# Low weight parts written by an accumulating DMA instead of a GpSimd subtraction, in a two-layer Hawk/HGRN2 step

## The chip, the cores and the metric

The kernel runs on one core of a Trainium2 chip. The metric is the device time of one execution in microseconds (us). Engines are named as the profile names them: PE (TensorE matmul), PEld (its weight loads), DVE (VectorE), ACT (ScalarE), POOL (GpSimd), SP (SyncE, which issues most DMAs here).

## What is computed

The reference runs one step of a two-layer decoder trunk on 1024 prompt tokens and 8 x 4 sample tokens (1056 in all), model width 1024, in float32:

```
# layer 0 (RG-LRU)
u = rmsnorm(x) @ w_in                  # 1024 -> 2 x 1536: xb and gate
xc = causal_conv(xb)                   # 4 taps
r, ig = sigmoid(blockdiag(xc) + b)     # 16 blocks of 96 x 96 each
h = scan(a, b)                         # h_t = a_t h_(t-1) + b_t, a = exp(-8 softplus(-lam) r)
x = x + (h * silu(gate)) @ w_out       # 1536 -> 1024
# layer 1 (HGRN2, 8 heads of 128 x 128 state)
q, f, v, gate = rmsnorm(x) @ w_in      # 1024 -> 4 x 1024
o = gated linear attention(q, f, v)
x = x + (rms(o) * silu(gate)) @ w_out
y = rmsnorm(x)
```

## The kernel before, in words

Activations lie transposed: features on the 128 partitions, the 1056 tokens along the free dimension, in three chunks of 352. Each float32 operand of a large product is split into a high part, rounded to the PE's fast format (F32R), and a low part, which is what rounding left over. `mm3` (lines 237 to 243) then makes one product out of three matmuls: high weight by high input (L241), high weight by low input (L242), low weight by high input (L243). So every weight block needs a high and a low copy before its matmuls run.

`weights` (L364) prepares a weight matrix in blocks of up to 512 columns: SP loads the block into one of three buffers `raw`, ACT copies it with rounding into one of four buffers `whi` (L376), and an engine subtracts `whi` from `raw` into one of four buffers `wlo` through `subtract` (L319; the instruction is at L321). The default engine is POOL (`G`). With four buffers and two blocks for a 1024-row product, the blocks of the next item are prepared while the present one is multiplied; a `raw` buffer is free for the next load when both its readers are done.

The callers of `weights` are the input products of layer 0 (`project0`, `by_chunk`, and the head `begin`, which names its engines itself), the two partial output products `out` (L623, 8 blocks of 384 columns each, beside loads and stores of the residual stream), `first1` and `ahead` at the end of layer 0, the first two heads of layer 1 (`HC = 2`), and the first part of the last output product. The other six heads go through `seven`, whose `split` (L1423) has its own subtraction on POOL. Two more places split weights by hand: `load` in `out_last` (L657, 18 subtractions on POOL) and the blocks `late` near the end (L1649, 8 subtractions of 384 columns).

The order of the work is made by the class `Flow`: each step is recorded with its engine, an assumed cost and the keys that it reads and writes. A list scheduler plans each of the two halves (layer 0, layer 1) and emits the instructions in the planned order; after that each engine runs its own list strictly in order, waiting on semaphores. The products of the main path keep their written order on PE; smaller PE work and all work of the other engines is placed by the plan. For layer 0 the plan is also improved by a seeded random search over its first 60 us. A changed cost or step therefore moves instructions in other places too.

In layer 1 the first heads overlap on DVE with `build` (L1342) and `add` (L1362, instruction at L1363), which form sums of input parts for `seven`, and with `scale` (L1031), which multiplies the decay factors into queries and keys. `own_gate` (L1058, instruction at L1061) starts a head's chain; `burst1` to `burst4` are its PE work (L1049 is the first). `parted_sum` splits the sums that `build` forms, with a subtraction on POOL (also L321, tiles `t<-R,t` and `t<-tmp,t`).

Of the kernel before, what the change touches and what calls it, by code (L numbers as in the profile page):

```python
# [14 lines left out]
F32 = mybir.dt.float32  # L15
# [3 lines left out]
AF = mybir.ActivationFunctionType  # L19
ALU = mybir.AluOpType  # L20
# [189 lines left out]
def tile_trunk(ctx: ExitStack, tc: tile.TileContext, xT, prm, hc, w0, wg, wo0, w1, wo1, s_in,  # L210
               yT, h_out, c_out, sp_out, ss_out):
    nc = tc.nc
    V, S, G, T, Q = nc.vector, nc.scalar, nc.gpsimd, nc.tensor, nc.sync
# [15 lines left out]
    def pc(name, j, n=1):  # L229
        a = PRM[name][0] + j  # L230
        return P[:, a:a + n]
# [4 lines left out]
    def chunk(c):  # L236
        return slice(c * CH, (c + 1) * CH)
# [56 lines left out]
    with ExitStack() as l0:  # L294
        pl = l0.enter_context(tc.tile_pool(name="l0", bufs=1, reuse_waits="tile"))
        fl = Flow("PE")

        def fixed(name, shape, dt=F32, pool=None):
            return (pool or pl).tile(shape, dt, tag=name, name=name)
# [7 lines left out]
        def dma(dst, src, r=(), w=(), prio=5, kb=180, q=Q):  # L307
            fl.add("SP" if q is Q else "ACT", 0.45, lambda: q.dma_start(dst, src), r, w, prio, kb * (1.0 if r else 0.75))

        def act(n, emit, r, w, prio=5, more=0.0):  # L310
            fl.add("ACT", 0.25 + 0.0007 * n + more, emit, r, w, prio)

        def dve(n, emit, r, w, prio=5, both=False):
            fl.add("DVE", 0.13 + 0.0011 * n, emit, r, w, prio, both=both)

        def pool(n, emit, r, w, prio=5):
            fl.add("POOL", 0.1 + 0.00245 * n, emit, r, w, prio)

        def subtract(e, n, b, x, a, r, w, prio):  # L319

            emit = lambda: e.tensor_tensor(b, x, a.bitcast(F32), op=ALU.subtract)  # L321
            if e is G:
                pool(n, emit, r, w, prio)
            else:
                dve(n, emit, r, w, prio, True)
# [35 lines left out]
            b = 6 * c + 2 * j + i  # L361
            return X[:, b * CH:(b + 1) * CH], ("X", b)

        def weights(src, n, prio=2, e=G, at=None, q=Q, own=()):  # L364

            own = iter(own)
            got = []
            for a in range(0, n, 512):
                m = min(512, n - a)
                raw, *rk = next(own, None) or next(raws)  # L370
                if at:
                    (hi, hk), (lo, lk) = ((o[:, a:a + m], k) for o, k in at)
                else:
                    (hi, hk), (lo, lk) = next(his), next(los)
                dma(raw[:, :m], src[:, a:a + m], (), rk, prio, m / 2, q)
                act(m, lambda hi=hi, raw=raw, m=m: S.copy(hi[:, :m], raw[:, :m]), rk, (hk,), prio)  # L376
                subtract(e, m, lo[:, :m], raw[:, :m], hi[:, :m], (*rk, hk), (lk,), prio)
                got.append((hi, lo, hk, lk))

            def get(k):  # L380
                q = slice((k % 4) * 128, (k % 4 + 1) * 128)
                hi, lo, hk, lk = got[k // 4]
                return hi[:, q], lo[:, q], (hk, lk)

            return get

        def product(w, xs, step=8, more=()):

            ps, pk = next(mm)
            n = len(xs)  # L390
            for s in range(0, n, step):
                ks = range(s, min(n, s + step))

                def emit(ks=ks):
                    for k in ks:
                        mm3(ps[:, :CH], w(k)[:2], *xs[k][:2], k == 0, k == n - 1)

                fl.add("PE", 0.48 * len(ks), emit, (*(q for k in ks for q in (*xs[k][2], *w(k)[2])), *more), (pk,), 1, main=True)
            return ps, pk

        def xcols(c):
            return [(xh[k][:, chunk(c)], xl[k][:, chunk(c)], (("xh", k, c), ("xl", k, c))) for k in range(KD)]
# [217 lines left out]
        def ycols(c):  # L620
            return [(YH[j][:, chunk(c)], YL[j][:, chunk(c)], (("yh", j, c), ("yl", j, c))) for j in range(3)]
# [24 lines left out]
        def out_last(src):  # L646

            blocks = [{} for _ in range(KD)]

            def load(m, k, n, hi, hks, lo, lks, kept=()):  # L650

                raw, rk = next(raws)
                u = 128 * n
                a, b = ("wl", m, 0, k), ("wl", m, 1, k)
                dma(raw[:, :u], wo0[m][:, 768 + 128 * k:768 + 128 * k + u], (), (rk,), 1, u / 2)
                act(u, lambda: S.copy(hi, raw[:, :u]), (rk,), (*hks, a), 1)
                pool(u, lambda: G.tensor_tensor(lo, raw[:, :u], hi.bitcast(F32), op=ALU.subtract), (rk, a), (*lks, b), 1)  # L657
                for i in range(n):
                    q = slice(128 * i, 128 * i + 128)
                    blocks[m][k + i] = hi[:, q], lo[:, q], (a, b, *kept)  # L660

            def tail(k):
                q = slice(2 * CH, 2 * CH + 256)
                return xh[k][:, q], (("xh", k, 2),), xl[k][:, q], (("xl", k, 2),)

            flat = [o.rearrange("p a b -> p (a b)") for o in (gh, gl)]
            for i in (0, 3):
                q = slice(128 * i, 128 * i + 384)
                load(4, i, 3, flat[0][:, q], (("gh", 0), ("gh", 4)), flat[1][:, q], (("gl", 0), ("gl", 4)))
            for m in range(4):  # L670
                for k in (0, 3):
                    spots = []
                    for i in range(2):
                        a = (2 * m + i) * 768 + 128 * k
                        spots += [X[:, a:a + 384], tuple(("X", b) for b in range(a // CH, (a + 383) // CH + 1))]
                    load(m, k, 3, *spots)
            for i in range(3):
                load(5, 2 * i, 2, *tail(3 + i))
            bufs = [next(his) for _ in range(2)], [next(los) for _ in range(2)]
            ring_ = lambda i, a, n: [o for b in bufs for o in (b[i][0][:, a:a + 128 * n], (b[i][1],))] + [[b[i][1] for b in bufs]]  # L680
            for i, k in ((0, 6), (2, 7)):
                load(6, i, 2, *tail(k))
            load(6, 4, 2, *ring_(0, 0, 2))
            load(7, 0, 2, *ring_(0, 256, 2))
            load(7, 2, 4, *ring_(1, 0, 4))
            ms = (4, 0, 1, 2, 3, 5, 6, 7), (4, 0, 1, 2, 3, 5, 6, 7), (6, 7, 5, 4, 0, 1, 2, 3)
            own = [next(xos) for _ in range(NXO)]
            spare = halves[0][:8], own + [halves[0][8]] + [halves[1][i] for i in (0, 3, 6, 1)], halves[0][:8]
            for c in range(NCH):
                acc = next(xbs)  # L690
                rows = []
                for i, m in enumerate(ms[c]):
                    ps, pk = product(blocks[m].get, ycols(c) + xcols(c)[:3], 1)
                    x, xk = spare[c][m]
                    dma(x, src[m][:, chunk(c)], ((2, m, c),), (xk,), 3)
                    dve(CH, lambda x=x, ps=ps: V.tensor_tensor(x, ps[:, :CH], x, op=ALU.add), (pk, xk), (xk,), 0)
                    dma(x1d[m][:, chunk(c)], x, (xk,), (("x1d", m, c),), 3)
                    squares(i, x, xk, acc)
                    rows.append((m, x, xk))
                bc, bk = norm(acc)  # L700
                for m, x, xk in rows:
                    scaled_parts(c, m, x, xk, bc, bk, pc("g1", m), ("P",), G if m % 4 == 3 else V, 4)
# [139 lines left out]
        raw = (halves[1][:8], [slots[i] for i in (1, 4, 7, 2, 5, 8)] + [halves[1][8], free[8]], free[:8])  # L842
# [82 lines left out]
    with ExitStack() as l1:  # L925
        p1 = l1.enter_context(tc.tile_pool(name="l1", bufs=1, reuse_waits="tile"))
        fl = Flow(side=0.4)
# [7 lines left out]
        at = fixed("attn", [128, 8, 128], F32, p1)  # L935
# [634 lines left out]
        for k in range(H):  # L1570
            if k < 4:
                olds = [("x", 1, k, x) for x in range(2)] + [("T", 1, i, k, x) for i in range(2) for x in range(2)]
            else:
                n, i = ((2, 0), (3, 0), (4, 0), (4, 1))[k - 4]
# [21 lines left out]
        own = []  # L1596
# [42 lines left out]
        nl = 128 * K2  # L1639
        late = []  # L1640
        for m in range(KD):
            row = (xh, xl)[m // 4][4 + m % 4]
            hi, lo, hk, lk = row[:, :nl], row[:, nl:2 * nl], ("late", m, 0), ("late", m, 1)
            for k in (hk, lk):
                inherit(k, [("x", p, m % 4, x) for p in (2, 3) for x in range(2)])
            raw, rk = next(raws)
            dma(raw[:, :nl], wo1[m][:, 128 * K1:], (), (rk,), 1, nl / 2)
            act(nl, lambda hi=hi, raw=raw: S.copy(hi, raw[:, :nl]), (rk,), (hk,), 1)
            pool(nl, lambda hi=hi, lo=lo, raw=raw: G.tensor_tensor(lo, raw[:, :nl], hi.bitcast(F32), op=ALU.subtract), (rk, hk), (lk,), 1)  # L1649
            late.append((hi, lo, (hk, lk)))  # L1650

        spare = []
# [54 lines left out]
        for a, n in OUT:  # L1707
            q = slice(a, a + n)
# [3 lines left out]
            for m in range(KD):  # L1712
# [5 lines left out]
                hi, lo, wk = late[m]  # L1718
# [97 lines left out]
```

## Time and profile before

| | |
|---|---|
| median of 3 runs | 1077.81 us (1077.65 to 1078.84) |
| the profiled execution, its own time | 1075.47 us |
| its span | 1073.7 us |
| granted TensorE clock, mean over the span | 0.996 |
| instructions | 25345 |
| busy: PE / PEld / DVE / ACT / POOL | 1053.0 / 1024.5 / 808.2 / 611.1 / 558.0 us |
| DMA | 103.05 MB, mean 96 GB/s |

The page counts an engine as busy from the start of an instruction to its end; matmuls overlap, so one that is 0.32 us long may follow the last after 0.16 us. Line numbers are those of the kernel. A tile's name without a number stands for all its buffers.

### The profile page before, as it was taken

What the parts mean: (1) busy time and instruction counts of PE and PEld (TensorE: products, weight loads), DVE (VectorE), ACT (ScalarE), POOL (GpSimd) and SP (SyncE); (2) the same over time, 40 slices, a digit from 0 to 9 for tenths busy, and PEclk for the clock granted to TensorE, in tenths of its full rate; (3) what the DMA queues carried; (4) which work ended last, traced back from release to release, by engine and by line L of the source; (5) the groups of instructions that cost most, each with busy time, mean ns of one, the idle gap of its engine ahead of it and who ended that gap; (6) DMA issues with size and microseconds to landing.
All of it is one profiled execution on the core that took longest, in us unless ns stands there. A gap on an engine that the chain in (4) does not pass through costs nothing.

```text
span 1073.7 us, 25345 instructions
## 1 busy us (share of the span) xinstructions
PE 1053.0 (98%) x9972; PEld 1024.5 (95%) x9972; DVE 808.2 (75%) x1535; ACT 611.1 (57%) x1395; POOL 558.0 (52%) x546
## 2 busy tenths in 40 slices
PE   9999999999999999999999998999999999999997
PEld 9999999999999999999998997999999999989996
DVE  8999996887997787283999997767768585774446
ACT  7578656867665964243364563747474655752323
POOL 3425353353543547455574854656566665541545
PEclk9999999999999999999999999999999999999998
DMA  9101112124832775240110121212121212354204
GB/s 302 59 27 43 56 49 71 58 61 126 271 104 66 222 252 176 103 131 34 60 51 24 49 92 43 100 43 91 35 92 41 91 44 80 116 169 160 85 1 162
DMA packets 70119, 103.05 MB, mean 96 GB/s; under 512 B 9200, under 2 KB 51184, under 8 KB 70000
## 3 DMA queue, kind: packets, MB, share of 16 engines
q1 hardware_dynamic: 67696, 98.67, 28.1%
q10 hardware_dynamic: 2304, 2.77, 0.8%
q8 instruction: 78, 1.28, 0.5%
q14 instruction: 41, 0.34, 0.1%
HBM read 71.05 MB, written 25.49 MB: 90 GB/s over the span
## 4 chain that ended last, share of the span: by engine, by line
PE 82%; DVE 14%; issue 1%; DMA 1%; ACT 1%; POOL 0%; SPq 0%; POOLq 0%; ACTq 0%; DVEq 0%
PE mm L241 23%; PE mm L242 22%; PE mm L243 22%; PE hg L1049 2%; DVE R L1363 1%; DVE R L1031 1%; PE hg L1266 1%; PE hg L565 1%; DVE tmp L1363 1%; PE hg L1158 1%; DVE a L1232 1%; PE hg L1268 1%; DVE sg L1031 1%; PE hg L241 1%; PE hg L242 1%
## 5 line engine op out<-in xcount | busy, mean ns | idle before, releaser
L241 PE MATMUL mm<-xh,whi 128*128 128x352 f32 (+1 forms) x1143 | 359.3, 314 | 7.2 <-DVE sg L1504 4.5
L242 PE MATMUL mm<-xl,whi 128*128 128x352 f32 (+1 forms) x1143 | 353.2, 309 | 0.0
L243 PE MATMUL mm<-xh,wlo 128*128 128x352 f32 (+1 forms) x1143 | 353.2, 309 | 0.0
L321 POOL TENSOR_TENSOR wlo<-wraw,whi 128x512 fp32r<-128x512 f32 (+2 forms) x131 | 175.9, 1351 | 168.7 <-ACT whi L376 83.6
L241 PEld LDWEIGHTS mm<-xh,whi 128*128 128x128 f32 x1143 | 214.7, 188 | 10.5 <-DVE sg L1504 6.0
L242 PEld LDWEIGHTS mm<-xl,whi 128*128 128x128 f32 x1143 | 215.0, 188 | 1.6 <-DVE xl L321 0.2
L243 PEld LDWEIGHTS mm<-xh,wlo 128*128 128x128 f32 x1143 | 214.9, 188 | 0.0
L497 DVE SCALAR_TENSOR_TENSOR k<-xb,prm_sb,k 128x352 f32<-128x352 f32 (+2 forms) x144 | 90.1, 637 | 10.9 <-ACT k L494 6.1
L241 PE MATMUL mm<-t,whi 128*128 128x264 f32 (+1 forms) x306 | 89.5, 293 | 0.0
L242 PE MATMUL mm<-t,whi 128*128 128x264 f32 (+1 forms) x306 | 87.7, 287 | 0.0
L243 PE MATMUL mm<-t,wlo 128*128 128x264 f32 (+1 forms) x306 | 87.5, 286 | 0.0
L580 POOL TENSOR_TENSOR k<-X 128x352 f32<-128x352 f32 x36 | 44.9, 1256 | 47.8 <-DVE R L581 38.6
L321 POOL TENSOR_TENSOR wlo<-R,whi 128x512 fp32r<-128x512 f32 x33 | 49.9, 1511 | 32.8 <-ACT whi L1423 28.9
L376 ACT CAST whi<-wraw 128x512 fp32r<-128x512 f32 (+2 forms) x83 | 46.0, 574 | 28.5 <-PE mm L242 16.9
L241 PEld LDWEIGHTS mm<-t,whi 128*128 128x128 f32 x306 | 57.6, 188 | 0.7 <-ACT k L1481 0.5
L1504 DVE TENSOR_TENSOR k<-mm,k 128x264 f32<-128x264 f32 x62 | 26.5, 430 | 41.5 <-PE mm L243 41.4
L243 PEld LDWEIGHTS mm<-t,wlo 128*128 128x128 f32 x306 | 57.7, 188 | 0.0
L242 PEld LDWEIGHTS mm<-t,whi 128*128 128x128 f32 x306 | 57.6, 188 | 0.0
L1031 DVE TENSOR_TENSOR R<-R,sg 128x512 f32<-128x512 f32 (+1 forms) x48 | 50.4, 1050 | 0.1
L241 PE MATMUL mm<-yh,whi 128*128 128x352 f32 x153 | 49.9, 326 | 0.0
L243 PE MATMUL mm<-yh,wlo 128*128 128x352 f32 x153 | 49.4, 323 | 0.0
L242 PE MATMUL mm<-yl,whi 128*128 128x352 f32 x153 | 49.4, 323 | 0.0
(415 smaller groups left out, 2684.6 us busy)
## 6 DMA issues: line engine op xcount, KB each, us to landing
wraw<-in_w_dram SPq DMA_DIRECT2D x91, 256.0 KB, 2.6
wraw<-in_wo_dram SPq DMA_DIRECT2D x34, 192.0 KB, 2.5
si<-in_s_in_dram SPq DMA_DIRECT2D x8, 512.0 KB, 4.2
out_ss_out_dram<-si SPq DMA_DIRECT2D x8, 512.0 KB, 2.6
sg<-x1b SPq DMA_DIRECT2D x21, 176.0 KB, 2.8
x<-sg SPq DMA_DIRECT2D x21, 176.0 KB, 1.8
R<-in_w_dram SPq DMA_DIRECT2D x14, 256.0 KB, 2.5
R<-td SPq DMA_DIRECT2D x72, 44.0 KB, 2.0
```

Of the source, the lines that this page charges most:

```text
L241: T.matmul(out, wh, xh, start=first, stop=False, skip_group_check=chained)
L242: T.matmul(out, wh, xl, start=False, stop=False, skip_group_check=chained)
L243: T.matmul(out, wl, xh, start=False, stop=last, skip_group_check=chained)
L321: emit = lambda: e.tensor_tensor(b, x, a.bitcast(F32), op=ALU.subtract)
L376: act(m, lambda hi=hi, raw=raw, m=m: S.copy(hi[:, :m], raw[:, :m]), rk, (hk,), prio)
L497: dve(u, lambda src=src, dst=dst, sh=sh, k=k: V.scalar_tensor_tensor(dst, sh(src, k), pc("cw", 12 * k + m), dst, op0=ALU.mult, op1=ALU.add ...
L565: fl.add("PE", 0.62, lambda ps=ps, i=i, c=c: T.matmul(ps[:96, :CH], gs[:, i, :], ST[:96, chunk(c)], start=True, stop=True), (("gs",), *((" ...
L580: pool(CH, lambda x=x, a=a, b=b: G.tensor_tensor(x, a.bitcast(F32), b.bitcast(F32), op=ALU.add), (ak, bk), (xk,), 3)
L1031: dve(n // 2, lambda sv=sv, dv=dv, s=s, f=f: V.tensor_tensor(dv[:, :, s, :], sv[:, :, s, :], f, op=ALU.mult), (*sk, *gk), dk if i == o els ...
L1049: T.matmul(ps[32 * j:32 * j + 32, n * w:n * w + w], B[:, o:o + 32], q(slice(o, o + 32)), start=True, stop=True, tile_position=(0, 32 * j))
L1363: dve(n, lambda: V.tensor_tensor(o, a, b, op=op), r, (w,), prio, True)
L1504: dve(QT, lambda: V.tensor_tensor(o[0], z[0], u[0], op=ALU.add), (z[1], u[1]), (o[1],), 0)
```

## The change

A new helper `low` replaces the subtraction on POOL in `weights` (where no engine is named) and for the `late` blocks. ACT writes the negated rounded block into the low buffer with one more activation, and POOL issues a DMA that adds the raw block to it in place: raw + (-rounded) is the low part. The DMA is planned at 0.93 us of POOL and half a KB for each column. The blocks of `out_last` keep a subtraction, on DVE instead of POOL. The splits in `seven`, those of the gate weights in `lru` (L543), and those with a named engine stay as they were.

```diff
+        def low(n, dst, src, r, w, prio=5):
+
+            act(n, lambda: S.activation(dst, src, AF.Copy, scale=-1.0), r, w, prio)
+            fl.add("POOL", 0.93, lambda: G.dma_start(dst.bitcast(F32), src, accum_op=ALU.add), (*r, *w), w, prio, n / 2)
+
...
-        def weights(src, n, prio=2, e=G, at=None, q=Q, own=()):
+        def weights(src, n, prio=2, e=None, at=None, q=Q, own=()):
...
                 act(m, lambda hi=hi, raw=raw, m=m: S.copy(hi[:, :m], raw[:, :m]), rk, (hk,), prio)
-                subtract(e, m, lo[:, :m], raw[:, :m], hi[:, :m], (*rk, hk), (lk,), prio)
+                if e is None:
+                    low(m, lo[:, :m], raw[:, :m], rk, (lk,), prio)
+                else:
+                    subtract(e, m, lo[:, :m], raw[:, :m], hi[:, :m], (*rk, hk), (lk,), prio)
...
-                pool(u, lambda: G.tensor_tensor(lo, raw[:, :u], hi.bitcast(F32), op=ALU.subtract), (rk, a), (*lks, b), 1)
+                subtract(V, u, lo, raw[:, :u], hi, (rk, a), (*lks, b), 1)
...
-            pool(nl, lambda hi=hi, lo=lo, raw=raw: G.tensor_tensor(lo, raw[:, :nl], hi.bitcast(F32), op=ALU.subtract), (rk, hk), (lk,), 1)
+            low(nl, lo, raw[:, :nl], (rk,), (lk,), 1)
```

In the program that results, POOL issues 92 such DMAs (60 of 512 columns, 24 of 384, 8 of 128) and ACT runs 92 activations more.

## The prediction

> **What bounds the kernel now.** I read the page first, for its busy times, slices and chain.
>
> ```profile
> PE 1053.0 (98%) x9972; PEld 1024.5 (95%) x9972; DVE 808.2 (75%) x1535; ACT 611.1 (57%) x1395; POOL 558.0 (52%) x546
> ...
> PE 82%; DVE 14%; issue 1%; DMA 1%; ACT 1%; POOL 0%; SPq 0%; POOLq 0%; ACTq 0%; DVEq 0%
> ```
>
> PE is busy in 98% of the span. The change adds and removes no matmul, so it can win at most what PE still waits: 1073.7 - 1053.0 = 20.7 us, and only that part which lies where weight blocks are prepared. POOL, which the change relieves, carries 0% of the chain. Second is DVE with 14%. The next view is the table by stage, then PE's waits.
>
> ```profile
> core 0: us, PE busy (x) PEld busy (x) DVE busy (x) ACT busy (x) POOL busy (x), PEclk, DMA share, GB/s
> ...
> 350.00:400.00 50.00, 50.00 (x305) 48.79 (x304) 41.84 (x66) 40.43 (x69) 25.11 (x19) 1.00 0.79 250
> ...
> 515.00:568.00 53.00, 50.76 (x682) 49.24 (x685) 51.64 (x93) 28.23 (x66) 33.07 (x30) 1.00 0.15 51
> ...
> 616.00:656.00 40.00, 36.09 (x510) 33.97 (x499) 38.36 (x63) 21.65 (x52) 23.31 (x19) 1.00 0.21 76
> ...
> PE hg L1049 <- DVE R L1061: 2.0, 1, 2.0
> ```
>
> In layer 0 (the row 350:400 stands for it) PE has no idle time: nothing can be won there, only lost. From 515 to 568 us, the first two heads of layer 1, DVE is busy in 51.64 of 53 us and PE idles 53 - 50.76 = 2.24 us, of which 2.0 are one wait, for `own_gate` (L1061), the last of a long row of DVE instructions. This is the one place where PE waits for an engine whose work the change touches. From 616 to 656 PE idles 3.91 us behind DVE too, but there POOL serves `seven`, which the change leaves alone.
>
> **What the change gives: DVE loses its collisions with POOL.** POOL's instructions from 515 to 568, grouped, and a few pairs in order of time:
>
> ```profile
> L321 POOL TENSOR_TENSOR t<-R,t 128x264 fp32r<-128x264 f32 x12 | 13.7, 1152 | 10.4 <-ACT t L1366 10.4
> L321 POOL TENSOR_TENSOR wlo<-wraw,whi 128x512 fp32r<-128x512 f32 x7 | 10.8, 1549 | 1.3 <-ACT whi L376 1.3
> L321 POOL TENSOR_TENSOR t<-tmp,t 128x264 fp32r<-128x264 f32 x10 | 9.0, 914 | 7.7 <-ACT t L1366 7.7
> ...
> 524.81 1.29 POOL L321 TENSOR_TENSOR wlo<-wraw,whi 128x512 fp32r<-128x512 f32 x1
> ...
> 525.50 1.17 DVE L1031 TENSOR_TENSOR R<-R,ST 128x528 f32<-128x528 f32 x1
> ...
> 527.25 1.76 POOL L321 TENSOR_TENSOR wlo<-wraw,whi 128x512 fp32r<-128x512 f32 x1
> ...
> 527.77 1.80 DVE L1031 TENSOR_TENSOR R<-R,sg 128x528 f32<-128x528 f32 x1
> ...
> 529.49 0.70 DVE L1031 TENSOR_TENSOR sg<-a,sg 128x528 f32<-128x528 f32 x1
> ...
> 540.61 2.73 POOL L321 TENSOR_TENSOR wlo<-wraw,whi 128x512 fp32r<-128x512 f32 x2
> ...
> 540.77 1.41 DVE L1363 TENSOR_TENSOR R<-xh,R 128x264 f32<-128x264 f32 x1
> ...
> 542.11 1.78 DVE L1031 TENSOR_TENSOR R<-R,sg 128x512 f32<-128x512 f32 x1
> ...
> 553.87 0.69 DVE L1031 TENSOR_TENSOR R<-R,sg 128x512 f32<-128x512 f32 x1
> ...
> 553.97 1.73 POOL L321 TENSOR_TENSOR wlo<-wraw,whi 128x512 fp32r<-128x512 f32 x1
> ...
> 554.48 1.52 DVE L1363 TENSOR_TENSOR R<-R,xh 128x264 f32<-128x264 f32 x1
> ...
> 556.03 0.43 DVE L1363 TENSOR_TENSOR R<-R,xl 128x264 f32<-128x264 f32 x1
> ```
>
> The same DVE instruction takes 0.70 us alone and 1.80 beside a POOL subtraction; at 512 columns 0.69 and 1.78; at 264 columns 0.43 and 1.41 to 1.52. Beside the seven weight subtractions of this stage the rows show these extensions: 1.17 - 0.70 = 0.47, 1.80 - 0.70 = 1.10, 1.41 - 0.43 = 0.98, 1.78 - 0.69 = 1.09, 1.52 - 0.43 = 1.09, together 4.7 us on the engine that sets the pace. The change takes all seven away. The 22 subtractions of `parted_sum` (13.7 + 9.0 us) stay and will go on colliding, perhaps at other instructions, so 4.7 is an upper figure; but PE can use only its own 2.24 us of waiting, under half of it. What is late next is PE itself: behind the gap there is only its own queue of products. Gain: 2.2 us.
>
> **What it costs, each with its cover.** Prices for one block:
>
> ```profile
> L376 ACT CAST whi<-wraw 128x512 fp32r<-128x512 f32 x61 | 36.9, 618 | 28.4 <-PE mm L242 16.9 <-DMA wraw<-in_w_dram 5.1 <-DMA R<-td 3.7
> ...
> L376 ACT CAST whi<-wraw 128x384 fp32r<-128x384 f32 x16 | 7.8, 512 | 0.1
> ...
> L1294 POOL TENSOR_TENSOR rst<-rst,mhalf 128x4 f32<-128x4 f32 (+1 forms) x24 | 21.4, 901 | 22.0 <-DVE rst L1292 22.0
> ...
> wraw<-in_w_dram SPq DMA_DIRECT2D x91, 256.0 KB, 2.6
> ...
> x<-sg SPq DMA_DIRECT2D x21, 176.0 KB, 1.8
> ```
>
> ACT: 60 blocks x 0.62 + 24 x 0.51 + 8 at about 0.3 (an estimate from these two by size) = 52 us. They lie mostly in stages like 350:400, where ACT has 9.6 of 50 us free and the four result banks that PE writes in turn cover a late eviction: a result waits until PE has filled the other three. Charge 0; without that cover each activation costs PE its own 0.6 us.
>
> POOL: the trace holds no DMA issued by POOL. Bounds: SP's issue of a block below (0.38 us, `276.60` further down) and a whole subtraction above, 1.55 us. I take 0.9, the price of POOL's smallest arithmetic instruction (L1294), since most of both is start and end. 92 x 0.9 = 83 us in place of 92 subtractions; POOL is at 52%, so charge 0. Behind the issue, POOL's queue holds the `parted_sum` subtractions and the steps that feed `own_gate`; an issue that waits for ACT's second activation holds them 0.6 us longer, yet it holds POOL itself 0.6 us less.
>
> Landing: the nearest rows are a load of 256 KB, 2.6 us, and a 176 KB transfer out of SBUF, 1.8 us. An accumulating DMA has to fetch the destination as well, so the bounds are 1.8 and twice 2.6 = 5.2; I take 2.6, the same size. A block is then ready later than now by the second activation 0.6 + issue 0.9 + landing 2.6 - subtraction 1.5 = 2.6 us (from 0.6 + 0.4 + 1.8 - 1.5 = 1.3 to 0.6 + 1.5 + 5.2 - 1.5 = 5.8). Does a block have that much time? I followed the 52 blocks that `weights` splits on POOL between 74 and 397 us from their subtraction to their first L243. The row at 321.57 stands for the usual case, and the others are two of the tightest:
>
> ```profile
> 278.26 4.62 POOL L321 TENSOR_TENSOR wlo<-wraw,whi 128x384 fp32r<-128x384 f32 x3 [1.60 <-ACT whi L376]
> ...
> 283.23 0.32 PE L243 MATMUL mm<-yh,wlo 128*128 128x352 f32 x1
> ...
> 321.57 1.53 POOL L321 TENSOR_TENSOR wlo<-wraw,whi 128x512 fp32r<-128x512 f32 x1 [0.87 <-ACT whi L376]
> ...
> 334.16 0.32 PE L243 MATMUL mm<-xh,wlo 128*128 128x352 f32 x1
> ...
> 391.07 1.33 POOL L321 TENSOR_TENSOR wlo<-wraw,whi 128x512 fp32r<-128x512 f32 x1 [0.20 <-ACT whi L376]
> ...
> 396.35 0.32 PE L243 MATMUL mm<-xh,wlo 128*128 128x352 f32 x1
> ```
>
> The usual block is done at 323.10 and used at 334.16, 11 us later. The first of the three subtractions from 278.26 ends near 279.8 (a third of 4.62 us) and its matmul starts at 283.23: 3.4 us. The last ends at 392.40 and is used at 396.35: 3.95 us. Both exceed 2.6: charge 0; at the upper bound 5.8 - 3.4 = 2.4 us and 5.8 - 3.95 = 1.85 us, one behind the other.
>
> DMA traffic: 60 x 256 + 24 x 192 + 8 x 64 KB = 21 MB more, a fifth of the present 103. In most stages that is nothing. In the two output products it is not:
>
> ```profile
> 280.00:290.00 10.00, 10.00 (x65) 10.00 (x64) 9.79 (x12) 2.74 (x5) 5.68 (x4) 1.00 0.97 295
> ...
> 380.00:390.00 10.00, 10.00 (x65) 10.00 (x64) 8.50 (x17) 4.87 (x10) 3.17 (x3) 1.00 0.93 298
> ...
> 390.00:420.00 30.00, 30.00 (x190) 30.00 (x189) 28.56 (x45) 18.55 (x38) 17.45 (x21) 1.00 0.61 193
> ...
> 276.60 0.38 SPq L308 DMA_DIRECT2D xb<-in_xT_dram  x1
> ...
> 285.21 0.49 DVE L632 TENSOR_TENSOR xb<-mm,xb 128x352 f32<-128x352 f32 x1
> ```
>
> The engines move 295 GB/s there at 97% busy. Eight blocks of 192 KB add 1.57 MB: 5.3 us of that capacity, or 10.7 if the fetched destination counts again. The residual load shown is issued at 276.60 and added at 285.21, 8.6 us later, of which it needs about the 2.6 of the load above: 6 us of lateness are covered. Charge 0; at the upper figure 10.7 - 6 = 4.7 us for each of the two products. SP's queue is in order: a load of `raw` waits until the DMA, not the subtraction, has read the buffer, and holds the residual loads behind it for as long.
>
> DVE receives the 18 subtractions of `out_last`, about 0.55 us each (between 0.43 and 0.69 above), 10 us in a stage around 390:420 where it is busy in 28.56 of 30. POOL's 18 end there, and with them extensions of 0.5 to 1.1 each, 9 to 20 us. Charge 0, at most 1 us. The head is planned anew by the random search: 45 of the 48 warm-up matmuls now stand first, 29 before. The work is the same; I give it 1 us in the range, on either side.
>
> [...]
>
> **Sum.** -2.2 + 0 = -2.2 us. The profiled execution took 1075.47 us (span 1073.7 and 1.8 around it), 2.3 below the median of 1077.81; I carry the difference over to the median: 1075.6 us.
>
> **Rivals.**
> 1. *Slower: the accumulating DMA lands late where the DMA engines are full.* Place: the two output products, in the rows 280:290 and 380:390, and the last block of `by_chunk` behind them. For it: 0.97 and 0.93 busy, and the 3.4 and 3.95 us above. Against: the usual block has 11 us. It decides from a landing of about 4 us or added DMA time of 6 us in one product. Price: 4.7 x 2 at the full upper bound of traffic, plus 2.4 + 1.85 of late blocks, 13.7 in all; when it happens half of it is likelier than all, 6.9 - 2.2 = +4.7: 1082.5 us.
> 2. *No change: the DVE stage stays as long as it is.* The 22 remaining subtractions move into the freed POOL time and meet other DVE instructions, or the first blocks of layer 1 come late and PE waits for them instead. It decides if DVE gains less than 2.2 of the 4.7 us. Time: 1077.8.
> 3. *More: DVE's lead beyond PE's need reaches the stage from 616 to 656.* It would have to survive 48 us in which DVE is not always busy; at most the 3.91 us of idle PE time go too. Half of it: 1075.6 - 2.0 = 1073.6.
>
> That the change does not do what it says is excluded: the instruction order holds the 92 DMAs and 92 activations.
>
> **Chances.** 0.2% (2.2 us) is about what a measurement of this kernel can tell from no change. Forecast 0.45: being at that edge, 0.28 of it counts as faster and 0.17 as same. Rival 1: 0.35, all slower. Rival 2: 0.08, 0.07 same and 0.01 slower. Rival 3: 0.12, faster. Faster 0.40, same 0.24, slower 0.36. Range: down to rival 3 with most of its idle time and the head's 1 us, 1072.5; up to rival 1 with its late blocks and most of its traffic, 1086. The forecast's own range is 1073.5 to 1077.5.
>
> **What would show it.** Right: PE's wait for L1061 near 566 gone; L1031 and L1363 on DVE shorter in the mean; PE at 10.00 of 10 in both output products. Wrong: a wait of L243, L241 or a DVE addition (L632 before) for a DMA around these two products, issues on POOL well over 1 us, landings over 4 us.

## The result, and the profile after

The changed kernel takes 1086.01 us (median of 4 runs, 1085.04 to 1087.9) against 1077.73 us before on the same chip (1077.18 to 1078.84): a ratio of 1.0079, 95% interval 1.0063 to 1.0095. It is 8.3 us slower; the forecast was 1075.6, 2.2 faster. The profiled execution of after took 1085.06 us with a span of 1083.2.

The page of after, those lines that answer to the ones of before, with the two largest DMA queues (q0 is POOL's) and the accumulating DMAs' median from issue to landing:

```profile
PE 1059.0 (98%) x9972; PEld 1030.5 (95%) x9972; DVE 767.8 (71%) x1553; ACT 655.7 (61%) x1487; POOL 492.6 (45%) x528
...
q1 hardware_dynamic: 67696, 98.67, 29.4%
q0 software_dynamic: 13248, 20.98, 11.7%
...
PE 85%; DVE 9%; DMA 3%; issue 1%; ACT 1%; SPq 0%; POOL 0%; ACTq 0%; POOLq 0%; DVEq 0%
...
wlo<-wraw POOLq DMA_DIRECT2D x58, 256.0 KB, 4.1
```

DVE and POOL are relieved as meant (808.2 to 767.8 us and 558.0 to 492.6), yet PE is busy 6 us longer with the same 9972 matmuls, and DMA has risen from 1% to 3% of the chain. The table by stage of after:

```profile
core 0: us, PE busy (x) PEld busy (x) DVE busy (x) ACT busy (x) POOL busy (x), PEclk, DMA share, GB/s
280.00:290.00 10.00, 10.00 (x61) 9.52 (x60) 8.03 (x15) 8.07 (x13) 5.20 (x6) 1.00 0.91 244
350.00:400.00 50.00, 48.58 (x292) 46.83 (x291) 29.71 (x55) 41.56 (x73) 15.11 (x17) 1.00 0.91 243
380.00:390.00 10.00, 10.00 (x64) 10.00 (x64) 7.66 (x12) 5.89 (x12) 1.75 (x2) 1.00 1.03 287
390.00:420.00 30.00, 27.90 (x163) 27.36 (x162) 19.89 (x44) 21.86 (x43) 3.40 (x5) 0.94 0.86 246
515.00:568.00 53.00, 53.00 (x671) 51.84 (x670) 44.69 (x93) 29.67 (x69) 27.77 (x32) 1.00 0.51 115
616.00:656.00 40.00, 37.65 (x528) 35.86 (x526) 39.51 (x63) 24.50 (x59) 25.15 (x21) 1.00 0.21 68
```

From 515 to 568 PE now has no idle time: the predicted gain is there. In 390:420, where before had none, PE idles 2.1 us and its granted clock is 0.94. PE's waits in after:

```profile
PE mm L241 <- DVE sg L533: 2.7, 1, 2.7
PE mm L241 <- ACT xh L1598: 2.4, 1, 2.4
PE mm L243 <- DMA wlo<-wraw: 2.1, 1, 2.1
PE mm L241 <- DVE k L1512: 1.7, 1, 1.7
```

and the first two of them before (the last two did not exist):

```profile
PE mm L241 <- ACT xh L1590: 1.4, 1, 1.4
...
PE mm L241 <- DVE sg L525: 1.0, 1, 1.0
```

Waits alone don't show where time is lost for good, so I also took the start of the n-th matmul in each trace, counted from the first one; PE's order is nearly the same in all of these kernels. The difference to the profiled execution of before, in us (its time, 1075.47, was itself 2.3 below its median, so all entries at the end look about 2 us worse than the medians do):

| at (us of before) | 79 | 389 | 405 | 537 | 567 | 655 | 940 | 993 | end |
|---|---|---|---|---|---|---|---|---|---|
| after | 1.6 | 3.9 | 7.9 | 8.2 | 6.0 | 6.9 | 7.1 | 9.8 | 9.9 |
| x1_layer0_sub | 0.1 | 0.1 | 0.1 | 0.0 | -2.3 | -0.5 | -0.4 | 2.4 | 2.9 |
| x2_layer1_sub | 3.5 | 6.3 | 8.5 | 8.8 | 7.8 | 7.6 | 8.0 | 9.4 | 9.9 |
| x3_price | 2.6 | 5.7 | 15.6 | 16.5 | 14.2 | 16.7 | 16.3 | 18.8 | 22.2 |
| x4_copy | 1.5 | 3.8 | 5.1 | 5.3 | 3.2 | 4.0 | 4.2 | 5.3 | 5.9 |
| x5_head1_only | 0.3 | 0.3 | 0.3 | 0.2 | -1.8 | -0.1 | -0.2 | 1.6 | 1.7 |
| x6_bychunk_sub | 5.3 | 7.1 | 7.2 | 7.6 | 5.5 | 6.2 | 6.4 | 9.0 | 9.4 |
| x7_after_seed2 | 1.4 | 3.7 | 7.7 | 7.6 | 5.5 | 7.1 | 7.0 | 10.2 | 10.3 |
| x8_before_seed2 | 3.0 | 4.6 | 4.7 | 5.2 | 5.1 | 5.1 | 5.2 | 5.3 | 5.6 |
| x9_out_sub | 1.1 | 2.9 | 3.0 | 3.5 | 1.3 | 2.0 | 1.9 | 4.3 | 4.4 |
| x10_head1_kb | 0.9 | 0.9 | 0.9 | 0.9 | -1.6 | -0.2 | -0.2 | 1.2 | 1.2 |
| x11_head1_pool | 0.0 | 0.0 | 0.0 | 0.1 | -2.2 | -2.8 | -2.8 | -0.7 | -0.7 |

The row of after splits the 9.9 us: 1.6 in the head; 2.3 between 79 and 389, most of it spread over all matmuls without a wait; 4.0 at one place near 397; 0.3 up to 537; a gain of 2.2 at 566; then 0.9 up to 655, 0.2 up to 940, 2.7 near 950 and 0.1 at the end. The experiments take these one by one.

**The place near 397.** The third block of `by_chunk` in before: its load (SP), its subtraction, and the first L243 that uses it:

```profile
377.93 0.52 SPq L308 DMA_DIRECT2D wraw<-in_w_dram  x1
...
386.24 1.68 POOL L321 TENSOR_TENSOR wlo<-wraw,whi 128x512 fp32r<-128x512 f32 x1 [3.03 <-ACT whi L376]
...
394.44 0.32 PE L243 MATMUL mm<-xh,wlo 128*128 128x352 f32 x1
```

The same block in after:

```profile
389.65 1.27 SPq L308 DMA_DIRECT2D wraw<-in_w_dram  x1
...
394.58 0.64 ACT L312 ACTIVATE wlo<-wraw 128x512 fp32r<-128x512 f32 x1 [0.56 <-DMA wraw<-in_w_dram]
...
395.61 0.87 POOL L313 DMA_DIRECT2D wlo<-wraw  x1 [7.85 <-ACT wlo L312]
...
400.69 0.66 PE L243 MATMUL mm<-xh,wlo 128*128 128x352 f32 x1 [2.10 <-DMA wlo<-wraw]
```

Before, the block was done at 387.92 and had 6.5 us to spare. After, it lands at about 400.6. PE itself is 3.9 us late here, so the block is 400.6 - 387.9 - 3.9 = 8.8 us late against PE. Of that its load is 389.65 - 377.93 - 3.9 = 7.8; the way from load to ready takes only 1.0 longer (11.0 against 10.0). The wait is 2.1 us by the end that the profile gives the matmul before it, and 2.3 counted from start to start, less the usual distance of 0.16. Behind the wait PE's granted clock halves, in windows of 2 us:

```profile
398.00:400.00 2.00, 0.58 (x4) 0.29 (x2) 0.17 (x1) 1.95 (x3) 0.00 (x0) 1.00 1.03 203
400.00:402.00 2.00, 1.31 (x4) 1.32 (x5) 0.00 (x0) 1.69 (x3) 0.00 (x0) 0.63 1.10 308
402.00:404.00 2.00, 2.00 (x8) 2.00 (x8) 0.00 (x0) 1.97 (x3) 0.00 (x0) 0.52 1.02 312
404.00:406.00 2.00, 2.00 (x14) 2.00 (x14) 1.78 (x3) 2.00 (x6) 0.00 (x0) 1.00 0.72 190
```

Eight matmuls in the third row where the fourth has 14. The record of the clock gives 3.413 us at half speed from 400.50 on, which costs half of it, 1.7 us: 2.3 of wait and 1.7 of clock are the 4.0.

### The profile page after: what moved, and what is told of

It is laid out like the page before. It is cut to its first block, busy times and chain, and to the rows that moved or that the text cites. A ratio compares the mean times of both kernels' runs of the same rounds, so it can differ in the third digit from the quotient of the medians.

```text
span 1083.2 us, 25545 instructions
## 1 busy us (share of the span) xinstructions
PE 1059.0 (98%) x9972; PEld 1030.5 (95%) x9972; DVE 767.8 (71%) x1553; ACT 655.7 (61%) x1487; POOL 492.6 (45%) x528
## 3 DMA queue, kind: packets, MB, share of 16 engines
q0 software_dynamic: 13248, 20.98, 11.7%
## 4 chain that ended last, share of the span: by engine, by line
PE 85%; DVE 9%; DMA 3%; issue 1%; ACT 1%; SPq 0%; POOL 0%; ACTq 0%; POOLq 0%; DVEq 0%
PE mm L241 24%; PE mm L243 23%; PE mm L242 23%; PE hg L1057 2%; PE hg L1274 1%; PE hg L1166 1%; DVE a L1240 1%; DMA wraw<-in_w_dram 1%; PE hg L1276 1%; PE hg L573 1%; DVE sg L1039 1%; PE hg L241 1%; PE hg L243 1%; PE hg L242 1%; DVE R L1039 1%
## 5 line engine op out<-in xcount | busy, mean ns | idle before, releaser
L241 PE MATMUL mm<-xh,whi 128*128 128x352 f32 (+1 forms) x1143 | 358.9, 314 | 7.7 <-DVE sg L1512 5.1
L243 PE MATMUL mm<-xh,wlo 128*128 128x352 f32 (+1 forms) x1143 | 355.1, 311 | 2.1 <-DMA wlo<-wraw 2.1
L242 PE MATMUL mm<-xl,whi 128*128 128x352 f32 (+1 forms) x1143 | 354.4, 310 | 0.0
L241 PEld LDWEIGHTS mm<-xh,whi 128*128 128x128 f32 x1143 | 215.3, 188 | 10.6 <-DVE sg L1512 6.6
L243 PEld LDWEIGHTS mm<-xh,wlo 128*128 128x128 f32 x1143 | 215.4, 188 | 2.4 <-DMA wlo<-wraw 2.4
L242 PEld LDWEIGHTS mm<-xl,whi 128*128 128x128 f32 x1143 | 216.0, 189 | 1.3 <-DVE xl L326 0.2
L313 POOL DMA_DIRECT2D wlo<-wraw x80 | 72.0, 946 | 130.8 <-ACT wlo L312 109.2
L326 POOL TENSOR_TENSOR wlo<-wraw,whi 128x512 fp32r<-128x512 f32 x51 | 69.3, 1363 | 66.4 <-ACT whi L1431 53.7
L241 PE MATMUL mm<-t,whi 128*128 128x264 f32 (+1 forms) x306 | 89.6, 293 | 0.7 <-ACT k L1489 0.7
L505 DVE SCALAR_TENSOR_TENSOR k<-xb,prm_sb,k 128x352 f32<-128x352 f32 (+2 forms) x144 | 78.0, 551 | 15.9 <-ACT k L502 8.1
L242 PE MATMUL mm<-t,whi 128*128 128x264 f32 (+1 forms) x306 | 87.6, 286 | 0.0
L243 PE MATMUL mm<-t,wlo 128*128 128x264 f32 (+1 forms) x306 | 87.5, 286 | 0.0
L588 POOL TENSOR_TENSOR k<-X 128x352 f32<-128x352 f32 x36 | 42.0, 1179 | 66.4 <-DVE R L589 61.3
L312 ACT ACTIVATE wlo<-wraw 128x512 fp32r<-128x512 f32 (+2 forms) x80 | 45.4, 585 | 32.8 <-PE mm L243 22.9
L241 PEld LDWEIGHTS mm<-t,whi 128*128 128x128 f32 x306 | 57.5, 188 | 1.2 <-ACT k L1489 0.9
L242 PEld LDWEIGHTS mm<-t,whi 128*128 128x128 f32 x306 | 57.7, 189 | 0.0
L243 PEld LDWEIGHTS mm<-t,wlo 128*128 128x128 f32 x306 | 57.6, 188 | 0.0
L1512 DVE TENSOR_TENSOR k<-mm,k 128x264 f32<-128x264 f32 x62 | 26.3, 428 | 37.1 <-PE mm L243 36.8
L241 PE MATMUL mm<-yh,whi 128*128 128x352 f32 x153 | 51.8, 338 | 0.3 <-DVE k L640 0.3
L243 PE MATMUL mm<-yh,wlo 128*128 128x352 f32 x153 | 49.4, 323 | 0.0
```

The costliest lines, as they stand in the source:

```text
L241: T.matmul(out, wh, xh, start=first, stop=False, skip_group_check=chained)
L242: T.matmul(out, wh, xl, start=False, stop=False, skip_group_check=chained)
L243: T.matmul(out, wl, xh, start=False, stop=last, skip_group_check=chained)
L312: act(n, lambda: S.activation(dst, src, AF.Copy, scale=-1.0), r, w, prio)
L313: fl.add("POOL", 0.93, lambda: G.dma_start(dst.bitcast(F32), src, accum_op=ALU.add), (*r, *w), w, prio, n / 2)
L505: dve(u, lambda src=src, dst=dst, sh=sh, k=k: V.scalar_tensor_tensor(dst, sh(src, k), pc("cw", 12 * k + m), dst, op0=ALU.mult, op1=ALU.add ...
```

## The experiments

**x1_layer0_sub: layer 0 back on POOL's subtraction.**

```
-                if e is None:
+                if e is None and fl.until is None:
                     low(...)
                 else:
-                    subtract(e, ...)
+                    subtract(e or G, ...)
```

`fl.until is None` holds in layer 1's plan alone.

> The blocks that `weights` splits in layer 0 go back to a subtraction on POOL; the accumulating DMA stays in layer 1, and the 18 subtractions of out_last stay on DVE. Matmul by matmul the changed kernel runs behind the one before by 1.6 us at 60 us, 3.9 at 390, 7.8 at 400, 6.0 at 567, 6.9 at 700 and 9.5 at the end. Theory A (the DMAs of layer 0 cost it, where the DMA engines are full): the 3.9 us at 397 and the 2.3 us between 60 and 390 go, the gain of 2.0 at 565 stays: 1086.0 - 6.2 = 1079.8, or 1078.2 if the head's 1.6 goes too. Theory B (layer 1's DMAs cost it, or the 18 subtractions on DVE): 1084 to 1086.

Measured: 1078.0 us (11 runs) against 1078.1, ratio 1.0001, interval 0.9993 to 1.001. The head, the slow spread and the place at 397 are all back to 0.1, so all that was lost up to 400 us came with the accumulating blocks of layer 0 or with the new plan that they bring (x8 tells these two apart); the 18 subtractions of `out_last`, still on DVE, cost nothing (0.1 at 405 and at 485). The gain at 566 is there, 2.3. It is lost again: a wait of 1.9 us (2.1 from start to start) for L1512 at 615 and two spells of half clock, behind 615 and behind 944.

**x2_layer1_sub: layer 1 back on POOL's subtraction.** The condition above turned round, and the last part of the output product through `subtract(G, ...)`.

> The reverse: layer 1's blocks go back to a subtraction on POOL, layer 0 keeps the accumulating DMA. Theory A: the losses up to 400 us stay (+7.8), the gain of 2.0 at 565 goes, and so do the 2.6 us lost around 950: about 1086.0 + 2.0 - 2.6 - 0.8 = 1084.6. Theory B: most of the loss goes, 1080 or less.

Measured: 1085.65 us, ratio 1.0081 (1.0066 to 1.0096). Theory A holds: without layer 1's accumulating DMAs the loss stays. In this trace 3.4 us of it are two spells of half clock, at 33 and 658 us; behind its wait at 400, of 1.9 us from start to start, there is none. Of the gain at 566 half is still there (8.8 to 7.8): PE comes 8 us late and waits 1.0 instead of 2.0.

**x3_price: the planner counts twice the bytes.**

```
-            fl.add("POOL", 0.93, lambda: G.dma_start(..., accum_op=ALU.add), (*r, *w), w, prio, n / 2)
+            fl.add("POOL", 0.93, lambda: G.dma_start(..., accum_op=ALU.add), (*r, *w), w, prio, n)
```

> The same kernel as the changed one, but the planner counts an accumulating DMA with twice the bytes (n instead of n/2 KB), since its packets were measured at 10.3 GB/s on an engine against 20.5 for the others. Theory C (the engines have the room, the planner only put the load of by_chunk's block too late): the wait of L243 for a DMA at 397 goes with its 3.9 us: about 1082. Theory D (no order helps while eight output blocks and by_chunk's blocks share full engines): within 1.5 us of 1086.0.

Measured: 1095.81 us, ratio 1.0169 (1.0155 to 1.0184). Both theories miss: the true price made it 10 us worse. The same block in this kernel, its negation, its issue and PE's wait:

```profile
399.14 0.61 ACT L312 ACTIVATE wlo<-wraw 128x512 fp32r<-128x512 f32 x1
...
400.16 0.87 POOL L313 DMA_DIRECT2D wlo<-wraw  x1 [1.55 <-PE mm L243]
...
407.40 0.66 PE L243 MATMUL mm<-xh,wlo 128*128 128x352 f32 x1 [6.51 <-DMA wlo<-wraw]
```

Its load went out at 391.50, against PE as late as in after (PE is 5.7 behind at 389 here, 3.9 there). What came on top is ACT: in after it negates the block as soon as the load has landed (394.58), here only at 399.14, 7.6 us after the load's issue, behind other work in its list. With the 6.5 us of wait came 10.2 us of half clock, 5.2 of them behind the wait's end. So a planner that thinks the accumulates hold the buffers longer does not load earlier, and the order that it writes for SP and ACT sets how late the block is.

**x4_copy: the same DMA without the add.**

```
-            fl.add(... G.dma_start(dst.bitcast(F32), src, accum_op=ALU.add) ...)
+            fl.add(... G.dma_start(dst.bitcast(F32), src) ...)
```

> The POOL-issued DMA only copies (no accumulate; the low part is then the raw block, so the products are other numbers), everything else including the order is the same. Theory A1 (fetching the destination makes these DMAs slow): the time of a 2 KB packet falls from 178 ns to about 90, landings from 4.1 to about 3 us, and the wait at 397 shrinks from 2.26 us to under 1 and with it the half clock of 3.4 us behind it: 1081 to 1083. Theory A2 (the price is the way through POOL's queue or the buffers it holds, not the add): within 1 us of 1086.0.

Measured: 1083.35 us, ratio 1.0057 (1.0044 to 1.007). Its queue and its landing from its page, and PE's wait at 397 from its waits:

```profile
q0 software_dynamic: 6592, 20.98, 5.2%
...
wlo<-wraw POOLq DMA_DIRECT2D x58, 256.0 KB, 2.6
```

```profile
PE mm L243 <- DMA wlo<-wraw: 0.9, 1, 0.9
```

The same 20.98 MB take 5.2% of the DMA engines instead of 11.7%, land in 2.6 us instead of 4.1, POOL's issue falls from 0.89 to 0.56 us (medians), and the wait falls to 0.9 with no half clock behind it. By the ratios the add is worth 0.0079 - 0.0057 of 1078, 2.4 us; the other 6.1 of the loss are not the add's. SP's list is the same as in after, and the third block's load goes out at 387.14, 2.4 us earlier against PE; that much of its 7.8 is the add's traffic, and the rest is not. In the table this row has the head and the spread of after (1.5 and 3.8) to 0.1 us, though its DMAs are twice as quick.

**x5_head1_only: the kernel before, with the accumulating DMA in head 1's eight blocks alone.**

```
-        def weights(src, n, prio=2, e=None, at=None, q=Q, own=()):
+        def weights(src, n, prio=2, e=G, at=None, q=Q, own=()):
...
-                    ws2[i] = weights(order[i][0], 1024)
+                    ws2[i] = weights(order[i][0], 1024, e=None)
```

with `out_last` and `late` on POOL as before.

> The kernel before, with the negation and the accumulating DMA only in the eight blocks that `weights` splits for head 1 of layer 1, the ones whose subtractions collided with DVE between 515 and 568 us; everything else, out_last too, subtracts on POOL. Theory A: the wait of 2.0 us for own_gate at 566 goes and no block of layer 0 or of the end moves: 2.2 us gained up to 600 us; if no new spell of half clock follows, 1078.1 - 2.2 = 1075.9. Theory E (PE only waits later what it gains there, since DVE is full up to 656, and half-clock spells follow PE's new waits): 1077.5 to 1078.5.

Measured: 1076.38 us (12 runs) against 1077.93, ratio 0.9988 (0.9979 to 0.9996): between the two theories. The gain of 2.1 at 566 is there, and 1.8 of it is waited out at 615:

```profile
618.68 0.39 PE L241 MATMUL mm<-xh,whi 128*128 128x264 f32 x1 [1.67 <-DVE k L1512]
```

DVE was not idle there: it had four sums L1371 in a row in its list ahead of this eviction, where before had one.

**x6_bychunk_sub: only by_chunk's four blocks back on POOL.** `weights(src, 1024, e=G)` in `by_chunk`.

> The changed kernel, with only the four blocks of by_chunk (the last projection of layer 0, loaded while the second output product writes its results) back on POOL's subtraction. Theory A (the accumulating DMA of its block lands too late, 6.0 us there against 4.1 in the middle): the wait of L243 for a DMA at 397 goes with the 2.26 us and the 1.7 us of half clock behind it: 1086.0 - 3.9 = 1082.1. Rival F (the block's load itself is late, held in SP's queue by the raw buffers of the blocks before it): the wait stays at L241 or L243 for another releaser, 1085 to 1086.5.

Measured: 1083.76 us, ratio 1.0054 (1.0037 to 1.007). The wait at 397 is gone with all its 4.0 us (7.1 at 389 and 7.2 at 405). By the ratios only 2.7 come back; the profiled execution had 6.8 us of half clock in the head that after's had not, which is 3.4 us. The third block's load still goes out 4.1 late against PE here (389.10 - 377.93 - 7.1).

**x7_after_seed2 and x8_before_seed2: another draw of the head's plan**, `Random(2)` for `Random(1)` in `search`.

> The changed kernel with another seed of the planner's random search, which only moves the first 60 us. Theory G (the 1.6 us lost in the head and the 2.3 us that PE's cadence loses between 60 and 390 us are chance of the plan): with the next run as its base, the difference in the head and in the cadence changes by over 1 us. Rival H (both come with layer 0's accumulating DMAs): +1.6 and +2.3 again. Time: 1083 to 1087.

> The kernel before with the same other seed. Theory G: its own head and cadence differ from those of the kernel before by over 1 us, 1076.5 to 1080. Rival H: within 0.7 us of 1078.1.

Measured: 1083.54 and 1082.64 us, ratios 1.0056 (1.0038 to 1.0074) and 1.0046 (1.0029 to 1.0062) to the kernel before. Theory G holds, by more than it asked: the kernel before, with nothing changed but the order of its first 60 us, loses 4.7 us. Its trace shows 3.0 us in the head (1.7 of them a spell of half clock) and 1.6 us of spread up to 389, as after does, without one accumulating DMA; and it still has the wait that the change was to remove:

```profile
PE hg L1049 <- DVE R L1061: 1.8, 1, 1.8
```

With the same draw the changed kernel is only 0.9 us slower than the unchanged one, and the two intervals overlap (four runs each). The two traces, 4.7 apart at the end of the table, are the slowest run of x7 and the fastest of x8.

**x9_out_sub: only the 16 blocks of the two output products back on POOL.** `weights(wo0[m]..., 384, e=G)` in `out`; `by_chunk` still accumulates.

> The changed kernel, with only the blocks of the two output products (16 of 192 KB) back on POOL's subtraction; by_chunk's four blocks keep the accumulating DMA. In the changed kernel the load of by_chunk's third block is issued at 389.65 us, 7.8 us later against PE's progress than before (377.93), its DMA is issued at 395.61 and lands 5.0 us later. Theory I (the lateness is mostly the load's: the output product's accumulates hold the raw buffers and fill the engines): the load goes out some 4 us earlier or more, the wait at 397 goes with its 3.9 us: about 1082. Rival (the landing of by_chunk's own DMAs alone is too long): the wait stays over 1 us, 1085 to 1086.

Measured: 1079.93 us (10 runs) against 1078.3, ratio 1.0022 (1.0012 to 1.0032): 6.1 us back. The third block of `by_chunk`, load and accumulating issue:

```profile
379.43 0.38 SPq L308 DMA_DIRECT2D wraw<-in_w_dram  x1
...
389.72 0.88 POOL L313 DMA_DIRECT2D wlo<-wraw  x1 [2.44 <-ACT wlo L312]
```

The load goes out 10.2 us earlier than in after, and PE waits for no block (2.9 at 389 and 3.0 at 405), though `by_chunk` accumulates as before. Theory I holds: the output product's accumulates in front made the load late. By x6 the accumulates of `by_chunk` itself are needed too, since the wait also goes when these alone are taken out.

How do they make it late? They do not hold the load up in the run. In after the third block takes the `raw` buffer of the block three loads before it, whose accumulating DMA is this one:

```profile
378.43 0.87 POOL L313 DMA_DIRECT2D wlo<-wraw  x1
```

It landed 4.8 us later, at 383.2, 6.4 us before the load goes out, and among SP's waits of after from 360 to 410 us there is none for an accumulating DMA. The load stands behind other transfers in SP's list. By the kernel's text the planner counts a buffer as held until the DMA has landed, and places the load by that; x3 and x9 agree, but no run changes this hold alone.

**x10_head1_kb and x11_head1_pool: x5's eight blocks in two other orders of layer 1.** In `low`, the planner's figures: `n / 8` for `n / 2`, and 1.35 for 0.93.

> The accumulating DMA only in head 1's eight blocks as in the run of that name, with the planner told that it moves n/8 KB instead of n/2, which only changes the order it writes for layer 1 (the first evictions L1512 of the seventh-products' stage stand ahead of the sums L1371 on DVE, nearer to the order of before). Theory E (PE's wait of 1.7 us for L1512 at 615 us is that order): the wait falls under 0.7 and the 2 us gained at 566 last to 655: 1075 to 1076 against 1076.4. Rival (DVE's work up to 656 us sets the time whatever the order): the gain is gone at 655 again, 1076 to 1078.

> The same eight blocks, with the planner told that the issue costs POOL 1.35 us (as much as the subtraction did) instead of 0.93; only the order of layer 1 changes. It is a second order for the same work. Theory E: as PE's waits between 600 and 655 fall or rise against the 4.6 us of the run with 0.93, the time follows, 1075 to 1077.5. Rival (DVE's work sets it): the sum of these waits stays within 0.7 us.

Measured: 1075.56 us, ratio 0.9971 (0.9961 to 0.9981), and 1075.17 us, ratio 0.9972 (0.9961 to 0.9984), against 1078.3. Theory E holds for the time. x11 is the clean case: the wait at 615 is gone and the lead of 2.2 at 567 is 2.8 at 655 and at 940. PE's waits over 0.3 us between 600 and 660, summed from the starts, are 4.4 before, 6.2 in x5, 3.4 in x10 and 3.2 in x11; so the order sets them, not DVE's amount of work. No run gives the kernel before another order in layer 1, so what the order alone is worth without the accumulating DMA is not shown. x10's lead goes at 647, in 6.8 us of half clock. x11's table by stage, for the stage of the gain and the one from 616:

```profile
515.00:568.00 53.00, 53.00 (x734) 51.46 (x733) 47.44 (x99) 32.83 (x75) 28.05 (x34) 1.00 0.40 92
616.00:656.00 40.00, 37.12 (x474) 35.86 (x473) 38.68 (x66) 21.33 (x51) 21.64 (x18) 0.96 0.18 61
```

These two are faster than both kernels of the study, by 2.7 and 3.1 us.

## Why the prediction was wrong

**The gain: right.** "Gain: 2.2 us": every kernel with the accumulating DMA in head 1's blocks gains 2.0 to 2.5 at 566. The reason holds too. DVE's forms from 515 to 568, before and then after:

```profile
L1031 DVE TENSOR_TENSOR R<-R,sg 128x512 f32<-128x512 f32 x5 | 5.1, 1010 | 0.0
L1363 DVE TENSOR_TENSOR R<-xh,R 128x264 f32<-128x264 f32 x4 | 3.8, 955 | 0.0
```

```profile
L1039 DVE TENSOR_TENSOR R<-R,sg 128x512 f32<-128x512 f32 x5 | 3.5, 709 | 0.1
...
L1371 DVE TENSOR_TENSOR R<-xh,R 128x264 f32<-128x264 f32 x4 | 1.7, 426 | 1.6 <-POOL t L326 1.6
```

1010 falls to 709 ns and 955 to 426, which is the uncollided time (0.69 and 0.43 us in before). "What is late next is PE itself" was wrong: 50 us further on the new plan makes PE wait 1.7 to 1.9 us for an eviction (x1, x5, after), and only another order (x11) keeps the gain.

**The prices of one block: half right.** POOL's issue, taken as 0.9:

```profile
L313 POOL DMA_DIRECT2D wlo<-wraw x80: 864/887/1229, 81.3 to 1018.1; - x80
```

0.89 us in the median, 1.23 at most. ACT's charge of 52 us is 655.7 - 611.1 = 45 and hidden. Landing, taken as 2.6, is 4.1 in the median and was 5.0 for the late block, inside the bounds of 1.8 and 5.2; but beside the two output products single blocks took up to 6.5 and 6.8, over the upper bound.

**The traffic: right as a price, too high as a danger.** Accumulated bytes moved at 10.3 GB/s on an engine, the others of the same run at 19.4 (20.5 before); a 2 KB packet took 187 ns against 84 in the median. That is the upper figure, with the destination counted again: the price of a byte about doubles, 1.9 times by these rates, and against the plain copies of x4 it is 11.7% of the engines against 5.2%, in 13248 packets against 6592. But the 4.7 us for each output product that were worked out from it, 9.4 in all, did not come: PE is at 10.00 of 10 in both output products (rows 280:290 and 380:390), as the forecast's charge of 0 had it. What the traffic did cost is in x4: a load 2.4 us later, a longer landing (4.1 us against 2.6), and about 2.4 us of time.

**The late block: the failed step.** The working asked how much later a block is ready than now (2.6, at most 5.8) and set that against each block's slack; the tightest were 3.4 and 3.95. The block that came late is another one, with 6.5 us of slack, and it was 8.8 late. 7.8 of these are its load, which the sum left where it was. The sentence "a load of `raw` waits until the DMA, not the subtraction, has read the buffer, and holds the residual loads behind it for as long" names the hold, and it was given no price. The hold came by way of the plan and not as a wait of SP in the run (x9); x4 puts 2.4 of the 7.8 us down to the add's traffic. Rival 1 therefore had the right place (the blocks of `by_chunk` behind the second output product) and nearly the right wait (1.85 against 2.3), by the wrong step.

**A wait cost more than its length.** Nothing in the prediction charged the half clock behind a wait, 1.7 us for each spell: one at 397 and one near 950, 3.4 of the 9.9 us between the two traces. It is not a sure cost: the wait of 1.9 us at 400 in x2 had no spell behind it. Nor does it set the two medians apart. The granted clock is 0.9946 in the mean of before's 54 runs beside the experiments (0.991 to 0.997) and 0.9945 in after's four, so before has such spells too; its trace, at 0.996, has only the one at its end. Of the 2.7 us lost near 950 the spell is 1.7; x5, x10 and x11 lose 1.4 to 2.1 there with no accumulating DMA nearby, so that loss is not put down to one.

**The head: right that it is planned anew, wrong in size.** "1 us in the range, on either side" was too small and too even. Six newly drawn plans (after's, which x2 and x4 share, and those of x3, x6, x7, x8 and x9) cost 1.1 to 2.6 us at 79 without their spells of half clock, and up to 5.3 with them; none was better than the old one. The 2.3 us of spread up to 389 were in no term. Together they are 3.9 of after's 9.9 us. That these are chance of the new plan is read from x8, which loses 4.6 up to 389 (1.7 of it a spell) by a new draw alone, and from x4, which loses the same 3.8 with plain copies.

So rival 1's sign was right, the forecast's gain was real, and the sum missed the load's lateness with the wait behind it and took one term (the new plan) at under half its size. The half clock, which it missed too, sets the two traces apart and not the medians.

## What to carry to other kernels

When a step keeps a buffer until a DMA has landed, price the next load into that buffer, not only the step itself: here a block with 6.5 us of slack was 8.8 late, 7.8 of it through its load, which the planner had put later. When an edit makes a planner write a new order, compare with the old kernel under a new draw too (x8), before the difference is put down to the edit. And try the edit where its gain lies and nowhere else: with eight blocks instead of 92, 8.3 us of loss became a gain of 1.6 to 3.1, by the order of layer 1.

## What the hardware showed that I had not expected

PE's granted clock falls to half behind some waits, for 3.413 us (in after from 400.50 and from 956.87) or two or three times that (6.8 in x6 and x10, 10.2 in x3). The starts keep to the same measure: within each trace the spells begin a whole number of such lengths apart (in after at 400.5, 956.9 and 1079.8 us, 163 and 36 lengths; in x1 at 618.7, 949.8 and 1072.7, 97 and 36). The length of a wait does not tell whether a spell follows: waits, counted from start to start, of 2.3 us (after, 397), 2.1 (x1, 615) and 1.9 (x7, 623) had one behind them, and waits of 2.86 (before, 646) and 3.38 (x4, 948) had none. My guess was that it depends on where a wait falls on the grid of these starts. Laid on the grid of its own spells, nearly all of the wait of after (398.4 to 400.7) lies in one length (397.1 to 400.5, PE busy 1.48 of 3.4 us), while an edge at 951.0 cuts that of x4 in two (1.55 and 1.89 busy), and one at 402.2 that of x2 at 400 (2.26 and 2.81). The guess is not borne out by all of them: before's length from 646.0 had 1.54 and no fall after it, and x1's from 946.4 had 1.73 and a fall. What decides stays open.

PE's back-to-back rate is not one number. From 60 to 390 us the mean distance of two 352-column matmuls that start without a wait is 160.6, 159.8 and 159.8 ns (L241, L242, L243) in before, x1 and x5, and 161.1, 160.4 and 161.2 in after, x2 and x4: equal to 0.1 ns within each group, whether the DMAs beside them accumulate or only copy. The groups differ by 0.8 ns in the mean; over the some 1900 matmuls from 79 to 389 us that is about 1.6 of the 2.3 us of spread, and the rest is in single longer distances. It changes with the head's plan (x8: 161.0, 160.6 and 161.0). What in the head decides it stays open.
